# A decoder block on one core: first loads on two DMA queues, both layer norm borders in a written order, and the second norm turned as the first

## Chip, core and metric

The kernel runs on one core of a Trainium2 chip. TensorE (PE, with its weight loads as PEld), VectorE (DVE), ScalarE (ACT), GpSimd (POOL) and SyncE (SP) each run their own queue in order and meet through semaphores. The metric is the device time of one execution in microseconds (us), lower is better.

## What is computed

One layer of a decoder block on 256 tokens of width 2048, in float32:

```python
mix = token_mixers(x, w_in[i], ...)               # linear attention + softmax attention, two branches
x = layer_norm(ALPHA * x + mix, ln1_g[i], ln1_b[i])
ffn = conv_gated_mlp(x, w_gate[i], w_up[i], conv_w[i], conv_b[i], w_down[i])
x = layer_norm(ALPHA * x + ffn, ln2_g[i], ln2_b[i])
x = x + jax.nn.sigmoid(x @ w_ple_gate[i]) * (p[i] @ w_ple_proj[i])
```

`layer_norm` takes mean and variance over the 2048 columns of a token, scales by a gain `g` and adds a bias `b` per column.

## The kernel before

**Split products.** A float32 value is used as two parts of the PE's reduced format: ACT copies `raw` into `hi`, DVE subtracts to get `lo`, and a product is three matmuls (hi by hi, lo by hi, hi by lo). Weights come as units of 128 x 2048 in the order of use (`wu`): unit 120 to 135 are the output projection `wo`, 136 to 223 gate and up, 224 to 267 the down projection `dn`, 268 to 283 the last gate `pg`. `prep` (line 158) issues one unit's two loads on SP, one ACT copy (line 107, through `copy`) and one DVE subtraction (line 171) for each half. `unit` (line 179) hands out a unit and prepares two ahead.

**Order.** Only SP's order is that of the program (`tc.manual_schedule`, line 109). On the other engines a scheduler orders the instructions at build time by priority (`tc.high_priority`) and by its own costs; `tc.keep_in_program_order` pins single ones. On the chip each engine then runs its list in order. PE too is written by hand inside `end1`.

**Start.** SP loads the transposed input (`load_x`, line 192) and the first weights `fv` (`fv_prep`, line 393, with loads and splits on lines 401 to 403) in turn: k-tile 0 of the input (128 x 256), the first weight tile in three pieces (384, 384 and 280 columns), k-tile 1, the next weight tile in three pieces, and then whole tiles of 524 KB. For each, ACT makes `hi`, DVE makes `lo`. PE runs nine warm-up products (line 117) and then the `fv` products (line 426): 18 for each of 16 k-tiles.

**The norm borders.** `residual` (line 921) adds a projection's result to the residual `z`, in two halves of 1024 columns and two token tiles t of 128. The last two units of the second half are its tail. As each of the four tail banks (t, c) ends, DVE adds it to `z` (line 934 or 932) and takes statistics (line 935). After the two banks of a token tile come a few 1-column operations (on DVE, and one power on POOL), then, for each of four column groups g of 512:

- norm: scale by mean and deviation. On ACT one instruction; or on DVE;
- turn: four 128x128 transposes on PE into one of **two** PSUM banks (`pmx`, line 68), gain and bias, then `hi` by ACT and `lo` by DVE into `x1T[g]` or `x2T[g]`, which the next products read.

In the first border (`ln_steps`, line 870) groups 0 and 2 (`AFF_DVE`) get gain and bias before they are turned, by two DVE instructions over 512 columns with the gains laid out along columns (`lnb`, lines 889 and 891), so that the turned bank is split directly (ACT copy, DVE line 785). Groups 1 and 3 are turned plain: after the transposes four 128-column instructions take turns on ACT (line 911) and DVE (line 913), one bank, one after the other; then the ACT copy and the DVE difference (line 916). In the second border (`ln_out`, line 836) all four groups are turned plain (lines 862 and 864), one is normed on DVE (line 849), three on ACT (line 852).

To cover the borders PE has other work: the tail of the second token tile, a small product `pp` of the per-layer embedding (24 products of 512 columns: `proj` in `end1`, `ple_proj` in the second border), and the first products of the next stage by token halves (`phase0` needs token tile 0 alone, `phase1` token tile 1; in the second border the head units of `pg`, whose k-tiles 0 to 3 lie in `x2T[0]`). After the second border `affine` (line 966) adds gain and bias to `z2` on DVE for the final residual, two passes a group.

Of the kernel before, what the change touches and what calls it, by code (L numbers as in the profile page):

```python
# [19 lines left out]
P = 128  # L20
D = 2048
S = 256
# [14 lines left out]
ZN_DVE = (0,)  # L37
AFF_DVE = (0, 2)
LN_ORDER = (1, 0, 3, 2)
# [7 lines left out]
DNW = (DNP, DNP[:-1])  # L47
WH = 1152
# [7 lines left out]
def tile_block(ctx: ExitStack, tc: tile.TileContext, wu, wfv, wpp, xT_in, x_in, pT_in, wlr,  # L56
# [53 lines left out]
    nc.scalar.preload_act_table_set("natural_log_exp_and_others")  # L110
# [5 lines left out]
    for _ in range(9):  # L116
        nc.tensor.matmul(pw_, lhsT=warm[:, 0:P], rhs=warm, start=True, stop=True)
# [5 lines left out]
    sums, half = {}, {}  # L123
# [34 lines left out]
    def prep():  # L158
        u = n_prep[0]
        n_prep[0] += 1  # L160
        if u in sums:
            prep_seven(u)
            return
        his, los = [], []
        for h in range(2):
            raw = ring.tile([P, 1024], F32, tag="raw", bufs=4, name=f"raw{u}_{h}")
            nc.sync.dma_start(raw, wu[u, :, h * 1024:(h + 1) * 1024])
            hi = w_tile("hi", F32R, f"hi{u}_{h}", u)
            copy(hi, raw)
            lo = w_tile("lo", F32R, f"lo{u}_{h}", u)  # L170
            nc.vector.tensor_tensor(lo, raw, hi.bitcast(F32), ALU.subtract)  # L171
            his.append(hi)
            los.append(lo)
        ready[u] = (his, los)
# [4 lines left out]
    def unit():  # L179
        u = n_used[0]  # L180
        n_used[0] += 1
        while n_prep[0] < min(NU, u + 3):
# [9 lines left out]
    def load_x(g, k0, k1, step=2):  # L192
        for k in range(k0, k1, step):
            e = slice(k, k + step)
            raw = t2("xraw").rearrange("p (k t) -> p k t", t=S)[:, 0:step, :]
            nc.sync.dma_start(raw, xT_in[:, 4 * g + k:4 * g + k + step, :])
# [127 lines left out]
    def x_half(name, act, K, evac, pulls=0, head=0, tail=0, mid=None, done=None, end=None,  # L324
               fine=False, ws=(), joined=None):
# [15 lines left out]
        for t in range(2):  # L341
            for i, w in enumerate(us):
                mm(i, w, (t,))
# [49 lines left out]
    def fv_prep(u, hs=(0, 1), his=None, los=None):  # L393
        his, los = his or [], los or []
        for h in hs:
            raw = wide.tile([P, WH], F32, tag="hi", name=f"fvraw{u}_{h}")[:, 0:NS]
            hi = s8([P, NS], F32R, name=f"fvhi{u}_{h}")
            lo = s8([P, NS], F32R, name=f"fvlo{u}_{h}")
            for o, n in fch if u == 0 else ((0, NS),):
                e = slice(o, o + n)  # L400
                nc.sync.dma_start(raw[:, e], wfv[u, :, h, e])
                copy(hi[:, e], raw[:, e])
                nc.vector.tensor_tensor(lo[:, e], raw[:, e], hi[:, e].bitcast(F32), ALU.subtract)
# [432 lines left out]
    def ln_out(zs, stats, t, act_out, cg, cb, nm, prio):  # L836

        z = zs[t]
        mv = sm.tile([P, 8], F32, tag="mv", name="mv")
        with tc.high_priority(P_STAT):  # L840
            nc.vector.bn_aggr(mv[:, 0:2], stats[t])
            nc.vector.tensor_scalar(mv[:, 2:3], mv[:, 1:2], LN_EPS, None, ALU.add)
            nc.gpsimd.tensor_tensor(mv[:, 3:4], mv[:, 2:3], mhalf, ALU.pow)
            nc.vector.tensor_scalar(mv[:, 4:5], mv[:, 0:1], -1.0, mv[:, 3:4], ALU.mult, ALU.mult)
        with tc.high_priority(prio):
            for g in range(4):
                zc = z[:, g * 512:g * 512 + 512]
                if g in ZN_DVE:
                    nc.vector.tensor_scalar(zc, zc, mv[:, 0:1], mv[:, 3:4], ALU.subtract,
                                            ALU.mult)  # L850
                else:
                    nc.scalar.activation(zc, zc, AF.Identity, scale=mv[:, 3:4], bias=mv[:, 4:5])
                pt = mxtile(f"pt{nm}{t}{g}")
                for i in range(4):
                    nc.tensor.transpose(pt[:, i * P:i * P + P], zc[:, i * P:i * P + P], ident)
                y = t2("lny").rearrange("p (k t) -> p k t", t=P)
                for i in range(4):
                    kt = 4 * g + i
                    gc, bc = chn[:, cg + kt:cg + kt + 1], chn[:, cb + kt:cb + kt + 1]
                    src = pt[:, i * P:i * P + P]  # L860
                    if i % 2:
                        nc.scalar.activation(y[:, i, :], src, AF.Identity, scale=gc, bias=bc)
                    else:
                        nc.vector.tensor_scalar(y[:, i, :], src, gc, bc, ALU.mult, ALU.add)
                hi = act_out[g][:, :, t * P:t * P + P]
                copy(hi, y)
                nc.vector.tensor_tensor(act_out[g][:, :, 256 + t * P:256 + t * P + P], y,
                                        hi.bitcast(F32), ALU.subtract)

    def ln_steps(zs, stats, t, act_out, gb_, cg, cb, nm):  # L870
# [13 lines left out]
        def norm(g):  # L884
            e = slice(g * 512, g * 512 + 512)
            zc = z[:, e]
            with tc.high_priority(P_LN1[t]):
                if g in AFF_DVE:
                    nc.vector.scalar_tensor_tensor(zc, zc, mv[:, 0:1], gb_[0][:, e],
                                                   ALU.subtract, ALU.mult)  # L890
                    nc.vector.scalar_tensor_tensor(zc, zc, mv[:, 3:4], gb_[1][:, e],
                                                   ALU.mult, ALU.add)
                else:
                    nc.scalar.activation(zc, zc, AF.Identity, scale=mv[:, 3:4], bias=mv[:, 4:5])

        def turn(g):
            zc = z[:, g * 512:g * 512 + 512]
            with tc.high_priority(P_LN1[t]):
# [22 lines left out]
    def residual(name, act, K, zs, stats, mid, done=None, end=None, ws=((), ())):  # L921

        for nh in range(2):
# [4 lines left out]
            def ev(t, c, ps, nh=nh, zp=zp):  # L928
                zc = zp(t, c)
                with tc.high_priority(P_STAT):  # L930
                    if ws[nh]:
                        nc.vector.tensor_tensor(zc, zc, ps, ALU.add)
                    else:
                        nc.vector.scalar_tensor_tensor(zc, zc, ALPHA, ps, ALU.mult, ALU.add)
# [66 lines left out]
    def ple_proj(half, w, pTs):  # L1001
        banks = [[[mmtile(f"pp{half}{t}{c}")] for c in range(2)] for t in range(2)]
        for k in range(2):
            o = slice(k * 1024, k * 1024 + 1024)
            x_mm(banks, (w[0][:, o], w[1][:, o]), pTs[k], (0, 1), k == 0, k == 1)
        return banks

# [12 lines left out]
    def end1(tail_mm):  # L1020
# [3 lines left out]
        with tc.manual_schedule(engines={mybir.EngineType.PE}):  # L1024
# [8 lines left out]
            def put(t):  # L1033
                for c in range(2):
                    o = t2("ppo")
                    copy(o, pb[t][c][0])
# [4 lines left out]
            def phase0(i):  # L1041
                us.append(unit())
# [11 lines left out]
            stat0, norm0, turn0 = ln_steps(z1, st1, 0, x1T, gain[0], c_g1, c_b1, "l1")  # L1054
            stat1, norm1, turn1 = ln_steps(z1, st1, 1, x1T, gain[0], c_g1, c_b1, "l1")
# [19 lines left out]
            turn0(G[3])  # L1075
            proj(1, 1)
            put(1)
            for i in range(3):
                phase0(i)
                turn1(G[i])  # L1080
                if i == 0:
                    for g in G[2:]:
                        norm1(g)
            for j in range(4):
                phase1(j)
                if j == 0:
# [5 lines left out]
                         [g for g in range(4) if g not in AFF_DVE]))  # L1092
# [95 lines left out]
    residual("dn", hT, NF, z2, st2, ({14: lambda: mid2(0), 15: lambda: mid2(1)}, {8: mid2a, NF // 2 - 5: mid2b}), done2, ws=DNW)  # L1188
# [4 lines left out]
    mixers.append(affine(z2, gain[1], lambda t: None))  # L1193
# [7 lines left out]
    for nh in range(2):  # L1201
        def ev_o(t, c, ps, ab=(0, 512), nh=nh):
# [13 lines left out]
               fine=nh == 1)  # L1216
# [36 lines left out]
def _layout(i):  # L1253
# [16 lines left out]
    wfv = wfv.reshape(8, 2, P, NS).transpose(0, 2, 1, 3)  # L1270
# [17 lines left out]
    return dict(wu=wu, wfv=wfv, wpp=_xst(i["w_ple_proj"][0]), xT=x.T.reshape(16, P, S).transpose(1, 0, 2),  # L1288
# [23 lines left out]
```

## Time and profile before

| | us |
|---|---|
| median of 3 runs | 1663.86 (1661.83 to 1664.18) |
| the profiled execution's own time | 1663.05 |
| its span in the trace | 1661.3 |
| PE busy | 1650.9 |
| DVE busy | 1193.2 |
| ACT busy | 865.4 |
| read from and written to HBM | 332.33 MB, 9.97 MB |

A row of the timeline gives the start in us from the start of the span, the busy time, the engine, the source line, the operation, output and inputs, shapes, the count of merged instructions, and in brackets the idle time of the engine before it with what ended it. Matmuls are pipelined: a row of n products lasts n starts plus the time of the last to come out.

### The profile page before, as it was taken

What the parts mean: (1) busy time and instruction counts of PE and PEld (TensorE: products, weight loads), DVE (VectorE), ACT (ScalarE), POOL (GpSimd) and SP (SyncE); (2) the same over time, 40 slices, a digit from 0 to 9 for tenths busy, and PEclk for the clock granted to TensorE, in tenths of its full rate; (3) what the DMA queues carried; (4) which work ended last, traced back from release to release, by engine and by line L of the source; (5) the groups of instructions that cost most, each with busy time, mean ns of one, the idle gap of its engine ahead of it and who ended that gap; (6) DMA issues with size and microseconds to landing.
All of it is one profiled execution on the core that took longest, in us unless ns stands there. A gap on an engine that the chain in (4) does not pass through costs nothing.

```text
span 1661.3 us, 24083 instructions
## 1 busy us (share of the span) xinstructions
PE 1650.9 (99%) x8984; PEld 1432.3 (86%) x8984; DVE 1193.2 (72%) x1751; ACT 865.4 (52%) x1245; POOL 62.8 (4%) x175
## 2 busy tenths in 40 slices
PE   9999999999999999999999999999999999999998
PEld 8988888888888888888888888888888888888787
DVE  6666658768756657775677777777777788887874
ACT  6745445445555544544465555555555555454733
POOL 0000000000000000000010000000000011010000
PEclk9999999999999999999999999999999999999999
DMA  7665555555555555667746666666666667695554
GB/s 295 232 201 183 165 188 181 177 179 177 184 178 174 173 189 194 194 195 283 235 150 209 231 232 205 206 211 205 205 209 205 202 246 271 223 345 208 183 192 168
DMA packets 95588, 343.87 MB, mean 207 GB/s; under 512 B 11064, under 2 KB 12736, under 8 KB 94064
## 3 DMA queue, kind: packets, MB, share of 16 engines
q1 hardware_dynamic: 90528, 324.51, 58.3%
q0 software_dynamic: 4944, 17.84, 2.8%
q8 instruction: 70, 1.15, 0.3%
q14 instruction: 46, 0.38, 0.1%
HBM read 332.33 MB, written 9.97 MB: 206 GB/s over the span
## 4 chain that ended last, share of the span: by engine, by line
PE 94%; DVE 2%; DMA 2%; ACT 1%; issue 1%; SPq 0%; POOL 0%; DVEq 0%; ACTq 0%
PE psu L237 9%; PE psg L237 9%; PE psm L237 7%; PE dn L281 7%; PE gr L281 5%; PE gv L281 5%; PE wo L281 5%; PE psu L239 5%; PE psg L239 5%; PE pg L281 4%; PE psm L239 4%; PE psa L237 3%; PE fv L426 2%; PE psfq L237 2%; PE psfk L237 2%; PE psq L237 2%
## 5 line engine op out<-in xcount | busy, mean ns | idle before, releaser
L107 ACT ACTIVATE hi<-raw 128x1024 fp32r<-128x1024 f32 (+1 forms) x568 | 593.0, 1047 | 629.2 <-issue 217.0
L171 DVE TENSOR_TENSOR lo<-raw,hi 128x1024 fp32r<-128x1024 f32 x534 | 653.1, 1225 | 358.1 <-ACT hi L107 357.1
L237 PE MATMUL psu<-x1T,hi 128*128 128x512 f32 x688 | 236.0, 389 | 0.0
L237 PE MATMUL psg<-x1T,hi 128*128 128x512 f32 x672 | 230.5, 389 | 0.0
L239 PE MATMUL psu<-x1T,lo 128*128 128x256 f32 x688 | 190.0, 276 | 0.0
L239 PE MATMUL psg<-x1T,lo 128*128 128x256 f32 x672 | 185.5, 276 | 0.0
L237 PE MATMUL psm<-xT,hi 128*128 128x512 f32 x512 | 175.8, 391 | 0.0
L237 PEld LDWEIGHTS psu<-x1T,hi 128*128 128x128 f32 x688 | 129.2, 188 | 26.7
L237 PEld LDWEIGHTS psg<-x1T,hi 128*128 128x128 f32 x672 | 126.2, 188 | 26.1
L239 PE MATMUL psm<-xT,lo 128*128 128x256 f32 x512 | 141.5, 276 | 0.0
L239 PEld LDWEIGHTS psu<-x1T,lo 128*128 128x128 f32 x688 | 129.1, 188 | 0.0
L239 PEld LDWEIGHTS psg<-x1T,lo 128*128 128x128 f32 x672 | 126.2, 188 | 0.0
L281 PE MATMUL dn<-hi,hT 128*128 128x512 f32 x432 | 121.4, 389 | 0.0
L237 PEld LDWEIGHTS psm<-xT,hi 128*128 128x128 f32 x512 | 96.2, 188 | 19.8
L239 PEld LDWEIGHTS psm<-xT,lo 128*128 128x128 f32 x512 | 96.2, 188 | 0.1
L281 PEld LDWEIGHTS dn<-hi,hT 128*128 128x128 f32 x432 | 81.0, 188 | 16.8 <-ACT hi L107 0.2
L237 PE MATMUL psa<-oT,hi 128*128 128x512 f32 x256 | 87.8, 389 | 0.0
L281 PE MATMUL gv<-hi,xT 128*128 128x512 f32 x256 | 72.3, 394 | 0.0
L281 PE MATMUL gr<-hi,xT 128*128 128x512 f32 x256 | 72.2, 394 | 0.0
L239 PE MATMUL psa<-oT,lo 128*128 128x256 f32 x256 | 70.7, 276 | 0.0
L281 PE MATMUL wo<-hi,mT 128*128 128x512 f32 x256 | 70.2, 390 | 0.0
L281 PE MATMUL dn<-lo,hT 128*128 128x512 f32 x216 | 68.9, 391 | 0.6 <-DVE lo L171 0.5
(300 smaller groups left out, 2806.2 us busy)
## 6 DMA issues: line engine op xcount, KB each, us to landing
raw<-in_wu_dram SPq DMA_DIRECT2D x568, 512.0 KB, 4.7
fvraw<-in_wfv_dram SPq DMA_DIRECT2D x14, 524.0 KB, 7.9
hi<-hsd POOLq DMA_DIRECT2D x17, 256.0 KB, 5.1
lo<-hsd POOLq DMA_DIRECT2D x17, 256.0 KB, 5.3
lnb<-in_lng_dram SPq DMA_DIRECT2D x4, 1024.0 KB, 9.0
hsd<-hsh POOLq DMA_DIRECT2D x9, 256.0 KB, 5.7
hsd<-hsl POOLq DMA_DIRECT2D x9, 256.0 KB, 5.5
z<-in_x_dram SPq DMA_DIRECT2D x2, 1024.0 KB, 8.5
```

The source lines that it names most:

```text
L107: nc.scalar.activation(o, i, AF.Copy, bias=0.0, scale=scale)
L171: nc.vector.tensor_tensor(lo, raw, hi.bitcast(F32), ALU.subtract)
L237: nc.tensor.matmul(ps, lhsT=hi[i // 8 if hoff == 0 else 0][:, w0 % 1024:w0 % 1024 + P], rhs=a[:, kt % 4, :], start=first and i == 0, stop= ...
L239: nc.tensor.matmul(ps[:, 256:512], lhsT=lo[i // 8 if hoff == 0 else 0][:, w0 % 1024:w0 % 1024 + P], rhs=a[:, kt % 4, 0:256], start=False, ...
L281: nc.tensor.matmul(bs[j][:, 0:m], lhsT=x, rhs=v[:, o:o + m], start=first and i == 0, stop=last and i == 2)
L426: nc.tensor.matmul(fbk[t][c][:, 0:n], lhsT=x, rhs=w[:, o:o + n], start=kt == 0 and i == 0, stop=kt == 15 and i == 2)
```

## The change

**Start.** The first weight tile now comes as its first 384 columns (`w0`), issued by ACT ahead of everything else there, while SP issues k-tile 0 (`x0`) and then one load of 920 columns (`w1`: k-tile 1 and the other 664 weight columns). The second weight tile is one load. The host lays these out in one array (`xw`), and lays `wfv` and `xT` out so that each load is one contiguous piece. Eight warm-up products stand in place of nine.

**First border.** The four tail banks run through without transposes between them, token tile 1's norms are pinned behind token tile 0's turns, the `lo` parts of units 137 and 138 are moved to written places, units 139 and 140 are prepared after the border, and the last turn stands one step later.

**Second border.** `ln_out` goes; `ln_steps` serves both. So groups 0 and 2 are scaled once by DVE before they are turned, groups 1 and 3 on ACT and turned plain. PE's order is written by hand there too: tail, then a quarter of `pp` and a turn of token tile 0, four times, then a head product of `pg` and a turn of token tile 1, four times. The norms of token tile 1 and the preparation of units 270 and 271 are pinned. `affine` for `z2` keeps to groups 1 and 3.

```diff
-ZN_DVE = (0,)
 AFF_DVE = (0, 2)
+PLAIN = (1, 3)
+LATE_LO = (137, 138)
+PIN = (270, 271)
+PIN_LO = (270, 271)
...
+    w0 = wide.tile([P, 1024], F32, tag="lo", name="w0")[:, 0:384]
+    nc.scalar.dma_start(w0, xw[256 * P:640 * P].rearrange("(p n) -> p n", n=384))
...
-    for _ in range(9):
+    for _ in range(8):
...
-    load_x(0, 0, 1, 1)
-    f0 = fv_prep(0, (0,))
-    load_x(0, 1, 2, 1)
-    fvu = [fv_prep(0, (1,), *f0)]
+    x0 = t2("xraw")[:, 0:256]
+    nc.sync.dma_start(x0, xw[0:256 * P].rearrange("(p n) -> p n", n=256))
+    w1 = wide.tile([P, 1024], F32, tag="lo", name="w1")[:, 0:920]
+    nc.sync.dma_start(w1, xw[640 * P:].rearrange("(p n) -> p n", n=920))
...
+    x_split(0, x0)
+    fv_split(*f0, w0, slice(0, 384))
+    fv_split(*f0, w1[:, 256:920], slice(384, NS))
+    x_split(1, w1[:, 0:256])
+    f1 = fv_prep(0, (1,))
...
-            for i in range(2):
-                tail_mm(1, 0, i)
-            tail_mm(1, 1, 0)
+            for c in range(2):
+                for i in range(2):
+                    tail_mm(1, c, i)
             turn0(G[0])
-            tail_mm(1, 1, 1)
+            proj(0, 0)
             turn0(G[1])
             stat1()
             for g in G[2:]:
                 norm0(g)
-            proj(0, 0)
+            proj(1, 0)
             turn0(G[2])
-            proj(1, 0)
-            put(0)
-            for g in G[:2]:
-                norm1(g)
             proj(0, 1)
             turn0(G[3])
+            norm1(G[0], keep)
+            norm1(G[1], keep)
+            put(0)
+            low(u1, 0)
+            norm1(G[2], keep)
             proj(1, 1)
             put(1)
...
-    def done2(t):
-        if t == 1:
-            pb.extend(ple_proj(1, *pq[0]))
-        ln_out(z2, st2, t, x2T, c_g2, c_b2, "l2", P_LN2[t])
+    def end2(tail_mm):
...
+        for g in range(2, 4):
+            norm0(g)
+        stat1()
...
+        for g, (k, t) in enumerate(((0, 0), (0, 1), (1, 0), (1, 1))):
+            proj(k, t)
+            turn0(g)
+        for g in range(4):
+            norm1(g, tc.keep_in_program_order)
+
+    def begin3(mm):
+        turn1, = late_turns
+        for g, (i, t) in enumerate(((0, 0), (1, 0), (0, 1), (1, 1))):
+            mm(i, t)
+            turn1(g)
+        border.close()
```

How the built programs order this, at three places. First the DVE queue in the first border, from token tile 1's last statistics on; `z_7195` (before) and `z_7184` (after) are token tile 1, `x1T_7196` to `x1T_7199` and `x1T_7185` to `x1T_7188` column groups 0 to 3. Before:

```order
L878 BN_AGGR mv<-st_85 128x2
L916 TENSOR_TENSOR x1T_7197<-lny,x1T_7197 128x4x128
L879 TENSOR_SCALAR mv<-mv 128x1
L785 TENSOR_TENSOR x1T_7196<-ptl_7850,x1T_7196 128x4x128
L881 TENSOR_SCALAR mv<-mv 128x1
L913 TENSOR_SCALAR lny<-ptl_7870,chn 128x128
L889 SCALAR_TENSOR_TENSOR z_7195<-z_7195,mv,lnb_7422 128x512 x2
L913 TENSOR_SCALAR lny<-ptl_7870,chn 128x128
L891 SCALAR_TENSOR_TENSOR z_7195<-z_7195,mv,lnb_7423 128x512 x2
L916 TENSOR_TENSOR x1T_7199<-lny,x1T_7199 128x4x128
L785 TENSOR_TENSOR x1T_7198<-ptl_7903,x1T_7198 128x4x128
```

After:

```order
L921 TENSOR_TENSOR x1T_7186<-lny,x1T_7186 128x4x128
L823 TENSOR_TENSOR x1T_7185<-ptl_7843,x1T_7185 128x4x128
L918 TENSOR_SCALAR lny<-ptl_7863,chn 128x128 x2
L921 TENSOR_TENSOR x1T_7188<-lny,x1T_7188 128x4x128
L823 TENSOR_TENSOR x1T_7187<-ptl_7881,x1T_7187 128x4x128
L893 SCALAR_TENSOR_TENSOR z_7184<-z_7184,mv,lnb_7411 128x512
L895 SCALAR_TENSOR_TENSOR z_7184<-z_7184,mv,lnb_7412 128x512
```

The four norm instructions of token tile 1 (line 889 and 891) stood between the third group's turned pieces and the last two differences of token tile 0; now all of token tile 0 stands ahead of the first pair, and the second pair follows later.

Second, the DVE queue in the second border after the change, from token tile 1's aggregate on; `z_12836` is token tile 1, `x2T_12838` to `x2T_12841` groups 0 to 3, `ptl_14709` the bank of token tile 0's fourth turn, `ptl_14773` that of token tile 1's first:

```order
L882 BN_AGGR mv<-st_12837 128x2
L823 TENSOR_TENSOR x2T_12838<-ptl_14665,x2T_12838 128x4x128
L883 TENSOR_SCALAR mv<-mv 128x1
L918 TENSOR_SCALAR lny<-ptl_14678,chn 128x128
L885 TENSOR_SCALAR mv<-mv 128x1
L180 TENSOR_TENSOR lo_1_14579<-raw_1_14575,hi_1_14577 128x1024
L918 TENSOR_SCALAR lny<-ptl_14678,chn 128x128
L921 TENSOR_TENSOR x2T_12839<-lny,x2T_12839 128x4x128
L823 TENSOR_TENSOR x2T_12840<-ptl_14696,x2T_12840 128x4x128
L918 TENSOR_SCALAR lny<-ptl_14709,chn 128x128 x2
L921 TENSOR_TENSOR x2T_12841<-lny,x2T_12841 128x4x128
L893 SCALAR_TENSOR_TENSOR z_12836<-z_12836,mv,lnb_14103 128x512
```

And before, from a little behind the same point; `z_12847` is token tile 1, `x2T_12849` to `x2T_12852` groups 0 to 3:

```order
L864 TENSOR_SCALAR lny<-ptl_14652,chn 128x128
L844 TENSOR_SCALAR mv<-mv 128x1
L867 TENSOR_TENSOR x2T_12849<-lny,x2T_12849 128x4x128
L864 TENSOR_SCALAR lny<-ptl_14652,chn 128x128
L864 TENSOR_SCALAR lny<-ptl_14665,chn 128x128
L867 TENSOR_TENSOR x2T_12850<-lny,x2T_12850 128x4x128
L849 TENSOR_SCALAR z_12847<-z_12847,mv 128x512
```

Token tile 1's norm of group 0 on DVE (one instruction, line 849) stood ahead of the last differences of token tile 0; now it is two (lines 893 and 895) and stands behind token tile 0's very last one.

Third, SP's first rows, before:

```order
L196 DMA xraw<-in_xT_dram 128x256
L401 DMA fvraw_0_128<-in_wfv_dram 128x384 x2
L401 DMA fvraw_0_128<-in_wfv_dram 128x280
L196 DMA xraw<-in_xT_dram 128x256
L401 DMA fvraw_1_144<-in_wfv_dram 128x384 x2
L401 DMA fvraw_1_144<-in_wfv_dram 128x280
L196 DMA xraw<-in_xT_dram 128x512
L401 DMA fvraw_0_160<-in_wfv_dram 128x1048
```

After, where ACT's first row is a load as well (`w_90`, 384 columns):

```order
L434 DMA xraw<-in_xw_dram 128x256
L436 DMA w_129<-in_xw_dram 128x920
L426 DMA fvraw_1_139<-in_wfv_dram 128x1048
L214 DMA xraw<-in_xT_dram 128x512
L426 DMA fvraw_0_149<-in_wfv_dram 128x1048
```

Ahead of the third weight tile (`fvraw_0_160`, now `fvraw_0_149`) SP issued nine loads, and now four.

More of the change, by code (lines that the diff above doesn't have):

```diff
@@ L121, in tile_block @@
     ready = {}
-    sums, half = {}, {}
+    sums, half, later = {}, {}, {}
     def prep_seven(u):
@@ L177, in tile_block, with unit @@
     NU = wu.shape[0]
-    def unit():
+    def unit(ahead=3):
         u = n_used[0]
         n_used[0] += 1
-        while n_prep[0] < min(NU, u + 3):
+        while n_prep[0] < min(NU, u + ahead):
             prep()
@@ L340, in x_half @@
         us = [unit() for _ in range(head)]
-        for t in range(2):
-            for i, w in enumerate(us):
-                mm(i, w, (t,))
+        if begin is not None:
+            begin(lambda i, t: mm(i, us[i], (t,)))
+        else:
+            for t in range(2):
+                for i, w in enumerate(us):
+                    mm(i, w, (t,))
         for i in range(head, n - tail):
@@ L834, in tile_block, with ln_steps @@
     ppd = dr.tile([2, P, 1024], F32, name="ppd")
[L836 to L870, printed above, removed]
+    def ln_steps(zs, stats, t, act_out, gb_, cg, cb, nm, prio):
         z = zs[t]
```

151 lines of the change are left out of this document (101 added, 50 removed).

## The prediction, made blind

> **What bounds the kernel now.** I read the shares of the span on the profile's first page, then what PE waited for by line, then the timeline at the three places that the change touches.
>
> ```profile
> span 1661.3 us, 24083 instructions
> PE 1650.9 (99%) x8984; PEld 1432.3 (86%) x8984; DVE 1193.2 (72%) x1751; ACT 865.4 (52%) x1245; POOL 62.8 (4%) x175
> ...
> PE fv L426 <- ACT fvhi L107: 1.7, 1, 1.7
> ...
> PE psg L250 <- DVE x1T L916: 1.1, 1, 1.1
> PE ptl L855 <- DVE z L849: 0.9, 1, 0.9
> PE dn L281 <- DVE lo L171: 0.5, 1, 0.5
> ```
>
> PE is busy 99% of the span and the change leaves its products as they are (one warm-up product less). So only PE's waits can move the time, and the list has them all in a few rows: one at the start, one in the first border, two in the second. What is to be won is about 5 us of 1663, and what can be lost is whatever new wait the written order makes.
>
> The prices of a product come from two rows of the chain of work (start, length, count): `fv` products have 384, 384 or 280 columns, those of `pg` 512.
>
> ```profile
> 13.62 39.12 PE fv L426 x246
> ...
> 1572.26 38.12 PE pg L281 x168
> ```
>
> A mean `fv` product costs 39.12/246 = 0.159, a 512-column product 38.12/168 = 0.227, and one of 256 columns half of that, 0.113.
>
> **A, the start.**
>
> ```profile
> 1.19 3.57 PE L117 MATMUL warm_ps<-warm 128*128 128x512 bf16 x9 [1.19 <-DVE warm L114]
> 2.92 0.42 ACT L107 ACTIVATE xT<-xraw 128x256 fp32r<-128x256 f32 x1 [0.58 <-DMA xraw<-in_xT_dram]
> 3.65 0.52 ACT L107 ACTIVATE fvhi<-fvraw 128x384 fp32r<-128x384 f32 x1 [0.32 <-DMA fvraw<-in_wfv_dram]
> 4.41 0.53 PE L426 MATMUL fv<-fvhi,xT 128*128 128x384 f32 x1
> ...
> 10.38 0.29 PE L426 MATMUL fv<-fvhi,xT 128*128 128x280 f32 x1
> 11.21 1.08 ACT L107 ACTIVATE fvhi<-fvraw 128x1048 fp32r<-128x1048 f32 x1 [1.17 <-DMA fvraw<-in_wfv_dram]
> 12.33 1.22 PE L426 MATMUL fv<-fvhi,xT 128*128 128x384 f32 x6 [1.66 <-ACT fvhi L107]
> 2.00:4.00 2.00, 2.00 (x6) 0.76 (x5) 0.43 (x1) 1.09 (x4) 0.00 (x0) 1.00 0.90 283
> 4.00:6.00 2.00, 2.00 (x11) 1.48 (x10) 1.12 (x2) 1.04 (x3) 0.00 (x0) 1.00 0.87 256
> 6.00:8.00 2.00, 2.00 (x15) 1.99 (x14) 1.70 (x4) 1.47 (x4) 0.00 (x0) 1.00 0.98 245
> 12.00:14.00 2.00, 1.60 (x8) 1.33 (x9) 1.63 (x2) 1.78 (x3) 0.00 (x0) 1.00 1.05 424
> ```
>
> (The last four rows are stretches of 2 us; their last column is what the DMA engines moved, in GB/s.) PE had done the 36 products of the first two k-tiles and stood still until the third weight tile had landed at 11.21 and been copied. From 13.62 on, 246 of the 288 products run without a gap. The six ahead of them, without a gap too, would start at 13.62 - 6 x 0.159 = 12.67: that is the effective start of k-tile 2 before.
>
> After, the first product comes at about 4.35: `x0` and `w0` are issued side by side and land at 3.3 to 3.7, near where ACT's copies found them before, and with eight warm-up products PE is free then. The 36 products take 36 x 0.159 = 5.72, and I add 0.5 for the wait on `w1`, now one load of 471 KB in place of three small ones. So k-tile 2 may begin at 10.6. Does its weight tile land in time? Up to its end 2,134 KB have to come. While the rows were of 1,024 to 1,536 bytes the engines moved 245 to 283 GB/s at a busy share of 0.87 to 0.98, and 424 at the same share when the rows were 4,192 bytes. After the change nearly all rows are 3,680 or 4,192 bytes: 566 KB in 2 to 4 us at the first stretch's 283, the other 1,568 KB at 424 in 3.7, thus landed near 8, copied by 9.2, no wait. A = 10.6 - 12.67 = **-2.0** (rounded up a little). Bounds: if no wait is left among the 36 products and the first comes at 4.1, -2.8; if the rate stays near 250, the tile lands at 2.0 + 2,134/250 = 10.5 instead of 11.21, -0.6.
>
> The Trainium skill's page "DMA: Bandwidth & Descriptors", section "Issuing engines are not separate DMA queues", speaks against the first half of this edit: transfers started by ScalarE, SyncE or GpSimd run on the same 16 engines and interleave, and starting them on several engines saves only the issue time, which it calls usually small. The rows above, with engines busy 0.87 and more from 2 us on, agree with it. By that rule the second queue alone is worth one issue on SP, and the rest of A must come from the larger rows.
>
> **B, the first border.**
>
> ```profile
> 836.95 0.42 PEld L901 LDWEIGHTS ptl<-ident,z 128*128 128x128 f32 x4 [0.50 <-ACT z L894]
> 840.69 0.42 PEld L901 LDWEIGHTS ptl<-ident,z 128*128 128x128 f32 x4 [0.30 <-DVE lny L913]
> 844.25 1.41 DVE L889 SCALAR_TENSOR_TENSOR z<-z,mv,lnb 128x512 f32<-128x512 f32 x2
> 845.89 1.41 DVE L891 SCALAR_TENSOR_TENSOR z<-z,mv,lnb 128x512 f32<-128x512 f32 x2
> 847.21 0.69 DVE L916 TENSOR_TENSOR x1T<-lny,x1T 128x512 fp32r<-128x512 f32 x1
> 847.96 1.35 PE L250 MATMUL psg<-x1T,hi 128*128 128x256 f32 x8 [1.13 <-DVE x1T L916]
> 849.50 2.13 PE L250 MATMUL psu<-x1T,hi 128*128 128x256 f32 x16
> ```
>
> Three waits: 0.50 before the first transposes, 0.30 for a PSUM bank, and 1.13 for `x1T` of the fourth group, which stood on DVE behind the four norm instructions of token tile 1 (1.41 + 1.41). Together 1.93. After, all of token tile 0 stands ahead of those four, and 24 products of 512 columns lie between the turns, so the 1.13 goes; the 0.50 goes as the whole tail of token tile 1 now stands before the first turn (6 x 0.227 = 1.36 more cover). The norms of token tile 1 come late instead: its first turn has `phase0`'s 48 products of 256 columns ahead of it, 48 x 0.113 = 5.4, against two instructions of 0.74, and its last one stands a `phase1` step later, which hides the late pair too. At the turns a bank wait stays: two banks for four turns, and ACT still has weight copies of 1.04 in its queue between the 128-column pieces. I take 0.6 for that, twice the 0.30 seen. B = 0.6 - 1.93 = **-1.3**, bounds -1.9 (nothing waits) and 0 (the bank waits take all back).
>
> **C, the second border.**
>
> ```profile
> 1556.06 1.06 ACT L107 ACTIVATE hi<-raw 128x1024 fp32r<-128x1024 f32 x1 [2.78 <-PE dn L281]
> 1558.48 1.09 PE L855 MATMUL ptl<-ident,z 128*128 128x128 f32 x8 [0.87 <-DVE z L849]
> 1559.47 0.72 DVE L864 TENSOR_SCALAR lny<-ptl,chn 128x128 f32<-128x128 f32 x2
> 1559.92 0.81 ACT L862 ACTIVATE lny<-ptl,chn 128x128 f32<-128x128 f32 x2 [0.28 <-DVE lny L864]
> ...
> L171 DVE TENSOR_TENSOR lo<-raw,hi 128x1024 fp32r<-128x1024 f32 x6 | 7.2, 1224 | 3.0 <-ACT hi L107 3.0
> ...
> L913 DVE TENSOR_SCALAR lny<-ptl,chn 128x128 f32<-128x128 f32 x8 | 3.3, 412 | 1.5 <-ACT lny L911 1.4
> ...
> L889 DVE SCALAR_TENSOR_TENSOR z<-z,mv,lnb 128x512 f32<-128x512 f32 x4 | 2.9, 746 | 0.0
> L891 DVE SCALAR_TENSOR_TENSOR z<-z,mv,lnb 128x512 f32<-128x512 f32 x4 | 2.9, 746 | 0.0
> ...
> L916 DVE TENSOR_TENSOR x1T<-lny,x1T 128x512 fp32r<-128x512 f32 x4 | 2.7, 674 | 0.7 <-ACT x1T L107 0.7
> L107 ACT ACTIVATE x1T<-lny 128x512 fp32r<-128x512 f32 x4 | 2.5, 630 | 0.5 <-DVE lny L913 0.5
> ...
> L862 ACT ACTIVATE lny<-ptl,chn 128x128 f32<-128x128 f32 x16 | 6.8, 468 | 0.3 <-DVE lny L864 0.3
> ```
>
> Before, PE loses the 0.87 of the `ptl` row here (the 0.5 at `dn` comes from a late weight load and stays). After, the whole tail of token tile 1 covers the first norm, so that 0.87 goes. But token tile 1's first norm, the DVE pair of lines 893 and 895, now stands behind the fourth turn's difference on DVE. The chain from the fourth turn's transposes: ACT piece 0.468, DVE piece 0.412, again 0.468 and 0.412, ACT copy 0.63, DVE difference 0.674, norm 0.746 and 0.746: 4.56, with eight hand-overs of about 0.04 (ACT's copy at 11.21 ended at 12.29 and PE began at 12.33) some 4.85. PE meanwhile has one head product, 12 matmuls of 512 columns, 12 x 0.227 = 2.72, and then needs that `z`: it stands 2.1, up to 2.6 if ACT first copies the third bank; I take 2.5. Behind PE at that point stand all head products of `pg`, so nothing else fills the hole. At the fourth turn's bank I expect 0.6 more: the second turn's pieces have a `lo` of 1.22 between them on DVE, about 3.8 in all, while two quarters of `pp` and one turn cover 2 x 6 x 0.227 + 0.42 = 3.14. C = 2.5 + 0.6 - 0.87 = **+2.2**. Bounds: all of it hidden -0.9; two late banks and 3.3 at the first turn +3.3.
>
> **The rest, at 0.** Eight passes fewer in `affine`, the moved `lo` parts and later units are on DVE, ACT and SP, behind which PE has two units in hand (two times 24 x 0.227); if that cover were gone, a `lo` would cost its 1.2. The tail of the program is as before. Sum: -2.0 - 1.3 + 2.2 = -1.1. The profiled execution took 1663.05 (its span 1661.3 and 1.75 around it), so 1661.95 for it; the median of the runs was 0.81 above it, so **1662.7**.
>
> **Rivals.**
>
> R1, the pieces do not alternate. In the rows at 1559.47 and 1559.92 DVE and ACT each run two pieces back to back, 0.72 and 0.81, in part side by side. If that holds for the fourth turn, the four pieces take about 0.85 instead of 1.9, the stall is 1.1, the bank wait goes, C = 1.1 - 0.87 = +0.2: 1663.86 - 3.1 = 1660.8; with nothing left, 1659.7. Against it, the first border:
>
> ```profile
> 849.78 0.46 ACT L911 ACTIVATE lny<-ptl,chn 128x128 f32<-128x128 f32 x1 [1.65 <-PE ptl L901]
> ...
> 851.13 0.46 ACT L911 ACTIVATE lny<-ptl,chn 128x128 f32<-128x128 f32 x1 [0.90 <-DVE lny L913]
> ```
>
> There ACT's second piece of one bank waited 0.90 for DVE's piece.
>
> R2, **slower than before**: in ACT's queue the copy of unit 269's second half stands ahead of every piece of the turns, and it waits for its load.
>
> ```profile
> 1550.63 1.06 ACT L107 ACTIVATE hi<-raw 128x1024 fp32r<-128x1024 f32 x1 [2.55 <-DMA raw<-in_wu_dram]
> ```
>
> A copy waited 2.55 for its load only 8 us ahead of the turns. If that copy is late, all turns are late by as much, with no other cover than the `pp` quarters; from 1.1 of lateness on the sum is positive, and at 2.55 it is +1.5: 1665.3. Against it: the copy at 1556.06 waited for PE, not for its load.
>
> R3, the start does not do what it says: the rate stays as it was, A = -0.6, sum +0.3: 1664.2. For it: the engines were already busy at 0.90 in the row of 2 to 4 us. Against it: 424 GB/s with long rows. The Trainium skill's section named above speaks for it too.
>
> **How the numbers follow.** The forecast, 1662.7, gets 0.60 (its own range 1660.8 to 1664.6), R1 0.21, R2 0.09, R3 0.10. The range reaches from R1's lower end, 1659.7, to a little above R2, 1665.6. A difference under 0.2%, 3.3 us, is about what a measurement of this kernel cannot tell from no change; so faster means under 1660.5 (nearly half of R1 and the forecast's good ends, A at -2.8 with B at -1.9: 0.22), slower above 1667.2 (R2 with bad ends: 0.05), and 0.73 is left for no change.
>
> **What would show it.** A: no gap of PE between 10 and 13 us, and `fv`'s chain ends at 50.7 instead of 13.62 + 39.12 = 52.74. B: the wait of `psg` for `x1T` is gone from the list. C: a wait of `ptl` for DVE's `z` of 2 to 3 us behind the first head product of `pg`. If that row is short, R1 holds; if a turn's pieces begin behind a copy that waits for a load, R2 does; if ACT waits for the third weight tile as late as 10 us, R3. Wrong altogether it would be if a wait stood anywhere between the borders.

## The result, and the profile after

The changed kernel takes **1665.99 us** (median of 20 runs, 1664.33 to 1668.72), the kernel before 1663.11 in the same runs (1661.83 to 1664.18): ratio **1.0019**, 95% interval 1.0012 to 1.0026. It is slower by 2.9 us. The forecast was 1662.7, 1.1 under the median then shown (1663.86, of three runs; the median of twenty is 0.75 lower); the time lies 0.4 over the range's upper end. The profiled execution after took 1665.31, 2.26 more than that of before.

The page's head and PE's waits by line, after:

```profile
span 1663.5 us, 24041 instructions
PE 1652.4 (99%) x8983; PEld 1433.0 (86%) x8983; DVE 1189.9 (72%) x1738; ACT 861.4 (52%) x1232; POOL 63.7 (4%) x175
...
PE ptl L906 <- issue: 2.7, 1, 2.7
PE dn L299 <- DVE lo L180: 1.0, 2, 0.7
PE ptl L906 <- DVE mv L883: 0.9, 1, 0.9
PE ptl L906 <- DVE lny L918: 0.3, 1, 0.3
PE dn1m L320 <- DVE ts L159: 0.2, 1, 0.2
PE ptl L906 <- DVE x1T L823: 0.2, 1, 0.2
```

The waits of before at `fv` and at `psg` are gone, and three of the transposes (`ptl`) have come, all in the second border. "issue" means that the profile found no releaser.

**Start.** The timeline of PE, ACT and DVE after:

```profile
4.28 0.82 PE L464 MATMUL fv<-fvhi,xT 128*128 128x384 f32 x1
5.36 0.84 PE L464 MATMUL fv<-fvhi,xT 128*128 128x384 f32 x2
7.05 1.08 ACT L110 ACTIVATE fvhi<-fvraw 128x1048 fp32r<-128x1048 f32 x1 [0.73 <-DMA fvraw<-in_wfv_dram]
8.16 1.25 DVE L416 TENSOR_TENSOR fvlo<-fvraw,fvhi 128x1048 fp32r<-128x1048 f32 x1 [0.93 <-ACT fvhi L110]
8.28 1.24 PE L464 MATMUL fv<-fvhi,xT 128*128 128x280 f32 x7
9.47 0.19 PEld L464 LDWEIGHTS fv<-fvlo,xT 128*128 128x128 f32 x1 [0.17 <-DVE fvlo L416]
```

The chain of work has all of `fv` in one row (start, length, count):

```profile
4.78 47.10 PE fv L464 x288
```

And two stretches by windows, with GB/s last:

```profile
4.00:6.00 2.00, 2.00 (x7) 1.42 (x5) 0.82 (x2) 0.97 (x3) 0.00 (x0) 1.00 0.94 344
6.00:8.00 2.00, 2.00 (x12) 2.00 (x12) 1.19 (x2) 1.27 (x3) 0.00 (x0) 1.00 1.03 400
```

The loads did get faster, 344 and 400 GB/s against 256 and 245 in the same stretches. But `fv` is done at 4.78 + 47.10 = 51.88 instead of 52.74: 0.86 earlier, not 2.0. The limit is now the *second* weight tile: it lands at 7.05, whole, is copied until 8.13 and subtracted until 9.41. PE's products of k-tile 1 begin at 8.41, right behind k-tile 0 (the last six of the row at 8.28; the first of it closes k-tile 0). These six need only the copy. The next one needs the difference and starts at 9.47, and the rest of `fv` follows it without another wait.

**First border.** One wait is left there, and it is the bank wait that was expected:

```profile
843.09 0.66 PE L906 MATMUL ptl<-ident,z 128*128 128x128 f32 x4 [0.18 <-DVE x1T L823]
...
869.90 0.39 PE L255 MATMUL psg<-x1T,hi 128*128 128x512 f32 x1
```

The second row is the 109th product of `psg`, a mark behind the border. Before, the same product started here:

```profile
872.04 0.39 PE L237 MATMUL psg<-x1T,hi 128*128 128x512 f32 x1
```

It comes 2.14 earlier; less the 0.86 of the start, the border gives 1.28.

**Second border.** PE, DVE and ACT, after:

```profile
1562.94 0.66 PE L906 MATMUL ptl<-ident,z 128*128 128x128 f32 x4 [0.89 <-DVE mv L883]
1565.33 0.66 PE L906 MATMUL ptl<-ident,z 128*128 128x128 f32 x4 [0.34 <-DVE lny L918]
1571.46 0.63 PE L906 MATMUL ptl<-ident,z 128*128 128x128 f32 x4 [2.70 <-issue]
1560.96 1.21 DVE L180 TENSOR_TENSOR lo<-raw,hi 128x1024 fp32r<-128x1024 f32 x1
1562.26 0.63 DVE L823 TENSOR_TENSOR x2T<-ptl,x2T 128x512 fp32r<-128x512 f32 x1
1563.74 1.21 DVE L180 TENSOR_TENSOR lo<-raw,hi 128x1024 fp32r<-128x1024 f32 x1
1569.22 0.69 DVE L921 TENSOR_TENSOR x2T<-lny,x2T 128x512 fp32r<-128x512 f32 x1 [0.69 <-ACT x2T L110]
1569.83 0.75 DVE L893 SCALAR_TENSOR_TENSOR z<-z,mv,lnb 128x512 f32<-128x512 f32 x1
1570.61 0.75 DVE L895 SCALAR_TENSOR_TENSOR z<-z,mv,lnb 128x512 f32<-128x512 f32 x1
1560.70 0.46 ACT L916 ACTIVATE lny<-ptl,chn 128x128 f32<-128x128 f32 x1 [1.05 <-PE ptl L906]
1563.30 0.46 ACT L916 ACTIVATE lny<-ptl,chn 128x128 f32<-128x128 f32 x1 [2.14 <-DVE lny L918]
1567.62 0.46 ACT L916 ACTIVATE lny<-ptl,chn 128x128 f32<-128x128 f32 x1 [0.84 <-DVE lny L918]
```

At 1571.46 PE waits 2.70 for token tile 1's first norm; the DVE pair at 1569.83 and 1570.61 ends at 1571.36, and it stands where the order had it, behind the fourth turn's difference at 1569.22. At 1562.94 the third turn waits 0.89 for its bank: the difference that empties it (1562.26) stands on DVE behind a `lo` of 1.21. (The row names line 883, a 1-column operation that DVE ran right behind that difference.) At 1565.33 the fourth waits 0.34 for the second turn's pieces, of which DVE's last stands behind the second `lo`. ACT's two pieces at 1560.70 and 1563.30 belong to one bank, and the piece at 1567.62 is the second of the fourth turn: the pieces do alternate.

The last `pg` product, started at 1655.32 before, starts at 1657.38. So 2.06 = -0.86 (start) - 1.28 (first border) + **4.20** (all behind it). Of the 4.20 the three waits are 3.93 less the 0.87 of before. Each wait also costs about 0.16 more than its idle time (from product start to product start the three are late by 1.06, 0.51 and 2.86), and there are two more of them than before; and the waits of `dn` for `lo` grew from 0.5 to 1.0. That makes about 3.9; the rest of the 4.20 is not accounted for.

### The profile page after: what moved, and what is told of

Read it like the earlier page. It is cut to its first block, busy times and chain, and to the rows that moved or that the text cites. A ratio compares the mean times of both kernels' runs of the same rounds, so it can differ in the third digit from the quotient of the medians.

```text
span 1663.5 us, 24041 instructions
## 1 busy us (share of the span) xinstructions
PE 1652.4 (99%) x8983; PEld 1433.0 (86%) x8983; DVE 1189.9 (72%) x1738; ACT 861.4 (52%) x1232; POOL 63.7 (4%) x175
## 4 chain that ended last, share of the span: by engine, by line
PE 94%; DVE 2%; DMA 1%; issue 1%; ACT 1%; POOL 0%; POOLq 0%; SPq 0%; DVEq 0%; ACTq 0%
PE psu L255 9%; PE psg L255 9%; PE psm L255 7%; PE dn L299 6%; PE gr L299 5%; PE gv L299 5%; PE wo L299 5%; PE pg L299 5%; PE psu L257 5%; PE psg L257 5%; PE psm L257 4%; PE psa L255 3%; PE fv L464 3%; PE psfq L255 2%; PE psfk L255 2%; PE psq L255 2%
## 5 line engine op out<-in xcount | busy, mean ns | idle before, releaser
L174 ACT ACTIVATE hi<-raw 128x1024 fp32r<-128x1024 f32 x534 | 564.7, 1060 | 598.2 <-issue 215.6
```

The source lines that it names most:

```text
L174: c = nc.scalar.activation(hi, raw, AF.Copy, bias=0.0, scale=1.0)
```

## Experiments

All times below are against the kernel before, run on the same chip; an interval is 95%. One 0.001 of ratio is 1.66 us. The changed kernel itself has 1.0019; where a run is set beside it, two such ratios are compared.

### Parts undone

**a1: the second border of before**, the other two parts changed. Edit (and what belongs to it: `ple_proj`, `affine` over all groups, no pins):

```diff
-    def end2(tail_mm):
...
-    def begin3(mm):
...
+    def done2(t):
+        if t == 1:
+            pb.extend(ple_proj(1, *pq[0]))
+        ln_out(z2, st2, t, x2T, c_g2, c_b2, "l2", P_LN2[t])
```

> The changed kernel with the second border of the kernel before (start and first border stay changed). Theory (the loss is all in the second border, the other two parts gain what the two traces show, 0.86 at the start and 1.16 at the first border): 2.0 us under before, ratio 0.9988, and PE's waits between 1530 and 1585 back at about 2.5 us in all. Rival (the parts disturb each other, or the gains of the profiled execution are chance): within 0.7 us of before.

Ratio 0.9997 (0.9988 to 1.0006). Its profiled span is 1660.0, and the waits in its second border are those of `ln_out`:

```profile
PE ptl L894 <- DVE z L888: 1.9, 2, 1.6
```

The loss against before is gone, so it was in the second border. The gain of 2.0 is not shown: it is the far end of the interval, and the medians differ by 0.14 alone, as the rival has it. Part of the reason stands in the row: its second border waits 1.9 for the norm, in two waits, where the kernel before waits 0.87, and 1.20 in its second profile (b0).

**b0: the kernel before, again.**

> The kernel before once more, for a second profile of its start. If the start of the one profile is typical, PE's third weight tile is waited for by 1.6 to 1.9 us again and the last fv product starts near 52.4; if executions differ there by more than 0.5 us, the 0.86 between the two first profiles is no measure of the change.

1663.94. Its chain of work has the row

```profile
13.75 39.12 PE fv L426 x246
```

`fv` done at 52.87, beside 52.74 (the wait for the third tile was only 0.8 this time, as PE came to it later). In eight profiles with the changed start and the whole second tile on two queues (the changed kernel twice, a1 to a4, b1, c5) it is done at 51.88, 52.56, 52.41, 52.21, 52.44, 52.76, 53.12 and 52.63: 52.5 in the mean. The second tile landed at 7.05 in the first of them and between 7.54 and 8.29 in the others. So the start gains about **0.3**, and the 0.86 of the first profile was a good draw. The gain of the first border, by contrast, is between 1.2 and 1.3 in every profile.

### The start

**a2: nine warm-up products.** Edit: `range(8)` to `range(9)`.

> The changed kernel with nine warm-up products, as before, in place of eight. In the trace after, the first fv products run 0.32 us apart for 384 columns until 6.5 us, in the trace before 0.17 to 0.18 from 5.1 us on. Theory W (the pause of PE between the eighth warm-up and the first product keeps PE slow): full speed from about 5 us, 1 us under the changed kernel, about 1.9 over before. Rival (the moment of full speed is a matter of chance or of when products pause later on): products slow until past 6 us again in the profile, time as the changed kernel, 2.9 over before.

Ratio 1.0011 (1.0002 to 1.002); the products were slow until 6.6 again. Over all profiles the slow first products come and go with eight warm-ups (slow in the changed kernel's first profile, a1 and a4, not in a3, b1 or c1) and with nine (slow in a2 and b0, not in the first profile of before). They do not set the end: a1 has them and is done at 52.41, a3 has not and is done at 52.44, as PE then only waits longer for k-tile 1. Theory W falls.

**b3: the second weight tile split in pieces.** One load still:

```diff
-            fv_split(hi, lo, raw, slice(0, NS))
+            for o, n in fch if (u, h) == (0, 1) else ((0, NS),):
+                fv_split(hi, lo, raw[:, o:o + n], slice(o, o + n))
```

> The changed kernel, but the second weight tile, still one load, is copied and subtracted in three pieces of 384, 384 and 280 columns, as before. Theory (the start lost its gain because k-tile 1's products wait for a copy of 1.08 and a subtraction of 1.25 of a whole tile that lands at 7.0 to 7.6): k-tile 1's first product at 7.6 to 8.1 in place of 8.4 to 9.1, fv done 0.4 to 0.8 earlier. Rival (PE's slow first products or the landing itself set the start): first product of k-tile 1 and end of fv as in the changed kernel, 51.6 to 52.4.

ACT in the timeline of this kernel (the three pieces as one row):

```profile
7.59 1.26 ACT L110 ACTIVATE fvhi<-fvraw 128x384 fp32r<-128x384 f32 x3 [1.64 <-DMA fvraw<-in_wfv_dram]
```

Its chain of work:

```profile
8.76 43.18 PE fv L465 x269
```

K-tile 1 starts at 8.16 and `fv` is done at 51.94, although the tile landed only at 7.59. The two other kernels with the pieces (c1, c2) are done at 51.61 and 51.60. Their mean is 51.7, 0.8 earlier than with the whole tile. Not all of this is the pieces: in c1 and c2 the tile also landed earlier than in most of the eight, at 7.23 and 6.70. With the same landing (7.60 in a3, 7.59 here) the end is 52.44 whole and 51.94 in pieces. So the theory holds, and the pieces are worth about 0.5; why the landing differs from execution to execution, no run shows. The time, 1.0012 (1.0003 to 1.0021), lies under the changed kernel's 1.0019, but the intervals overlap.

**b4: one queue.** `w0` is issued by SP behind `x0`:

```diff
-    nc.scalar.dma_start(w0, xw[256 * P:640 * P].rearrange("(p n) -> p n", n=384))
...
+    nc.sync.dma_start(w0, xw[256 * P:640 * P].rearrange("(p n) -> p n", n=384))
     w1 = wide.tile([P, 1024], F32, tag="lo", name="w1")[:, 0:920]
```

> The changed kernel, but w0 is issued by SP behind x0, so that one queue makes all first loads. Theory (the second queue saves one issue of about 0.4, and that is hidden behind the wait for the second weight tile): first fv product up to 0.4 later, k-tile 1's first product and the end of fv as in the changed kernel, time the same. Rival (two queues make the loads themselves faster): landings of w1 and of the second weight tile later by more than 0.5, fv done more than 0.5 later.

PE's first product in the timeline, and `fv` in the chain of work:

```profile
4.22 0.67 PE L464 MATMUL fv<-fvhi,xT 128*128 128x384 f32 x1
```

```profile
10.36 42.42 PE fv L464 x264
```

The first product is not later (4.22; 4.28 to 4.45 with eight warm-ups and two queues), `fv` is done at 52.78, within what two queues gave. Ratio 1.0016 (1.0007 to 1.0025), as the changed kernel. No use of the second queue can be seen. This agrees with the Trainium skill ("DMA: Bandwidth & Descriptors", section "Issuing engines are not separate DMA queues"), by which a second issuing engine saves only the time of issuing.

### The second border

**a3: the norm earlier.**

```diff
             proj(k, t)
+            if g == 3:
+                norm1(0, tc.keep_in_program_order)
             turn0(g)
-        for g in range(4):
+        for g in range(1, 4):
             norm1(g, tc.keep_in_program_order)
```

> The changed kernel, but token tile 1's first norm (two DVE instructions) is pinned ahead of the fourth turn's pieces instead of behind its difference. Theory (the stall of 2.7 us before token tile 1's first turn is that place in DVE's queue): the stall falls to 0.3 to 1.0, 2 us under the changed kernel, about 0.9 over before. Rival (DVE has no room in this border whatever the order): what is taken from that wait comes back at the next turns or at the fourth turn's bank, within 0.7 of the changed kernel.

Ratio 0.9994 (0.9985 to 1.0003). PE and DVE:

```profile
1569.55 0.63 PE L906 MATMUL ptl<-ident,z 128*128 128x128 f32 x4 [0.61 <-issue]
1567.72 0.74 DVE L893 SCALAR_TENSOR_TENSOR z<-z,mv,lnb 128x512 f32<-128x512 f32 x1
1568.70 0.74 DVE L895 SCALAR_TENSOR_TENSOR z<-z,mv,lnb 128x512 f32<-128x512 f32 x1
```

The pair now runs between the fourth turn's pieces and ahead of its difference. The wait falls from 2.70 to 0.61, with the same two waits at the third and fourth turn (0.90 and 0.34). One place in DVE's queue was worth 2.1 us of the trace. The time came down to that of before, where 0.9 over it was expected; c4 has a part of the reason.

**a4: unit 269's `lo` later**, behind token tile 1's first norms (through the kernel's own list `LATE_LO`).

```diff
-LATE_LO = (137, 138)
+LATE_LO = (137, 138, 269)
...
             norm1(g, tc.keep_in_program_order)
+            if g == 1:
+                for rest in later[269]:
+                    with tc.high_priority(P_LN2[1]):
+                        tc.keep_in_program_order(rest())
```

> The changed kernel, but both lo parts of unit 269 stand on DVE behind token tile 1's first norm, not between token tile 0's turns. Theory (the 0.9 to 1.06 at the third turn and the 0.3 to 0.5 at the fourth are banks held because of these two subtractions of 1.2): both waits go, the stall before token tile 1's first turn stays near 2.7, and up to 0.5 comes at the second head product's lo; 1 to 1.5 us under the changed kernel. Rival (the banks wait for ACT's pieces or token tile 1's statistics): both waits stay above 0.7 in sum, within 0.5 of the changed kernel or slower, as lo is then late.

Ratio 1.001 (1.0001 to 1.0019).

```profile
1563.74 0.66 PE L906 MATMUL ptl<-ident,z 128*128 128x128 f32 x4 [0.47 <-DVE lny L918]
...
1569.87 0.84 PE L906 MATMUL ptl<-ident,z 128*128 128x128 f32 x4 [2.72 <-issue]
```

The third turn's wait is gone, the fourth's is 0.47, in sum 0.47 for 1.23; the stall stays at 2.72. The `lo` parts did hold the banks. By ratio the gain over the changed kernel is 1.5 us, as expected, but the intervals overlap; the profiled execution lost some of it behind the stall, see c4.

**b1: both, with one `lo` ahead of the norm.**

```diff
+            if g == 3:
+                low(0)
+                norm1(0, tc.keep_in_program_order)
             turn0(g)
+        low(1)
```

> The changed kernel with token tile 1's first norm ahead of the fourth turn's pieces, and unit 269's lo parts moved: the first ahead of that norm, the second behind the fourth turn's difference. Theory (DVE's work in this border is near what PE's cover leaves, so that moving lo only moves the wait): the waits at the third and fourth turn fall from 1.6 to 0.6, that before token tile 1's first turn rises from 0.7 to about 1.2; the border within 0.5 us of the kernel with the early norm alone. Rival (the two remedies add): another 1.0 to 1.5 us less than with the early norm alone, then under before.

Ratio 0.9994 (0.9985 to 1.0003), as a3.

```profile
1569.70 0.63 PE L906 MATMUL ptl<-ident,z 128*128 128x128 f32 x4 [1.72 <-issue]
```

The two bank waits together are 0.1, for 1.24 in a3, and the stall has grown from 0.61 to 1.72: what was taken there came back here. The border of the changed kernel as one stretch by windows (busy times of PE, PEld, DVE, ACT, POOL):

```profile
1557.00:1571.40 14.40, 10.53 (x53) 7.85 (x51) 12.11 (x23) 8.33 (x15) 0.55 (x1) 1.00 0.26 83
```

DVE is busy 12.1 of 14.4 us, PE 10.5 (the other 3.9 are its three waits): here DVE's queue, not PE's, is the longer one.

**c2: more cover on PE.** With b1's early norm and b3's pieces (the second `lo` now ahead of the fourth turn's difference), both head products of token tile 0 stand ahead of the first two turns of token tile 1:

```diff
-        for g, (i, t) in enumerate(((0, 0), (1, 0), (0, 1), (1, 1))):
-            mm(i, t)
-            turn1(g)
+        mm(0, 0)
+        mm(1, 0)
+        turn1(0)
+        turn1(1)
+        mm(0, 1)
+        turn1(2)
+        mm(1, 1)
+        turn1(3)
```

> The changed kernel with the pieces at the start, the early norm, unit 269's lo parts on both sides of that norm, and PE's order in the second border changed: both first-half head products ahead of token tile 1's first two turns, so that 24 instead of 12 matmuls cover its norm. Theory (the loss is cover against DVE's chain): the stall before token tile 1's first turn falls to 0.5 or less, a new wait of 0.3 to 1.0 for its split comes before the next head product, the second border as before within 0.7; 1 to 2 us under before. Rival (DVE's queue is late by itself): the stall stays over 1.5.

Ratio **0.999** (0.9982 to 0.9999).

```profile
1569.43 0.74 PE L299 MATMUL pg<-lo,x2T 128*128 128x512 f32 x2 [1.00 <-DVE lo L180]
...
1571.76 0.73 PE L299 MATMUL pg<-hi,x2T 128*128 128x512 f32 x2 [0.25 <-ACT x2T L110]
```

No turn waits for the norm any more, and the split costs 0.25 (the fourth turn still waits 0.46 for its bank). The 1.00 in its place is DVE again: PE has reached the second head unit's `lo` before DVE has. The three waits sum to 1.71, as much as b1's 1.72 and more than the 0.87 and 1.20 of before. From the 109th `psg` product to the last of `pg` this kernel takes 785.64, and the kernel before 783.28 and 784.02 in its two profiles. So the stall went as forecast, but the stretch did not come back to that of before: the wait moved on to `lo`, and the gain in time is that of the start and the first border. (Three things differ from b1 here, so the cover alone is not measured.)

**c5: a longer queue.** Both `lo` parts pinned between the fourth difference and the norm:

```diff
+        for rest in later[269]:
+            with tc.high_priority(P_LN2[1]):
+                tc.keep_in_program_order(rest())
         for g in range(4):
             norm1(g, tc.keep_in_program_order)
```

> The changed kernel with both lo parts of unit 269 pinned ahead of token tile 1's first norm, behind the fourth turn's difference: it lengthens the stall by two subtractions of 1.2. Theory (the stall is the length of DVE's queue between the fourth turn and the norm): stall 2.9 + 2.4 = 5.3, the waits at the third and fourth turn down to 0.6 as when lo stood elsewhere, so 1 to 2 us over the changed kernel; and if a longer idle time always slows PE, seven or more head products 0.427 apart behind it, another 1.4 to 3. Rival (the stall is not that queue): stall near 2.9.

Ratio 1.0029 (1.0018 to 1.0041).

```profile
1572.51 1.09 PE L906 MATMUL ptl<-ident,z 128*128 128x128 f32 x4 [5.02 <-issue]
```

5.02 for 2.70: 2.3 more, which is two subtractions of 1.2. The stall follows the length of that queue.

**c4: the changed kernel, again.**

> The changed kernel once more, for a second profile. In its first profile the head products behind the stall of 2.9 run 0.227 us apart; with the stall as long, two other kernels had eight of them 0.427 apart. If that is chance in each execution, this profile shows the one or the other with the same waits ahead of it; the time is 2 to 4.5 us over before.

1666.92. PE behind the same stall, in the timeline:

```profile
1571.68 0.63 PE L906 MATMUL ptl<-ident,z 128*128 128x128 f32 x4 [2.74 <-issue]
1572.06 1.08 PE L299 MATMUL pg<-hi,x2T 128*128 128x512 f32 x2
1572.94 1.05 PE L299 MATMUL pg<-lo,x2T 128*128 128x512 f32 x2
1573.79 1.91 PE L299 MATMUL pg<-hi,x2T 128*128 128x512 f32 x4
```

The stretch by windows (the granted clock stands third from the end):

```profile
1572.00:1575.00 3.00, 3.00 (x10) 2.40 (x9) 2.22 (x4) 2.92 (x5) 0.00 (x0) 0.53 0.00 0
```

The granted clock is 0.53 and eight products start 0.427 apart instead of 0.227: 8 x 0.2 = 1.6 us on top of the stall. With stalls of 2.70 to 2.74, three profiles have this (c4, a4, b3) and three do not (the first of the changed kernel, a2, b4). The 20 runs of the changed kernel point the same way: the 5 with a mean granted clock of 1.000 took 1665.3 in the mean, the 15 with 0.999 or 0.998 took 1666.6. That is why the median after, 2.9 over before, can lie above the first profile's 2.3. The profiles of a3, b1 and c2, without such a stall, show no such products.

**c1: the parts that gained.** a1 and b3 together.

> The two parts that gained, without the one that lost: changed start with the second weight tile split in three pieces, changed first border, second border as before. By the traces so far: fv done 0.3 to 0.9 earlier, first border 1.25 less, second border 0: 1.6 to 2.1 us under before, ratio 0.9988 to 0.9990. Rival: executions differ more than that and the ratio is 1.000 within its interval.

Ratio **0.999** (0.9982 to 0.9999). Its second border waits 1.85 once:

```profile
1556.50 1.09 PE L895 MATMUL ptl<-ident,z 128*128 128x128 f32 x8 [1.85 <-DVE z L889]
```

That is 1.0 more than in the first profile of before at the same place and 0.65 more than in its second, which takes back part of what the start and the first border give; why it is longer, no run shows. c1 and c2 are both under both kernels, by 1.3 to 1.7 us against before (medians 1662.56 and 1662.45 for 1663.89, ratio 0.999); their intervals end just under 1.

## Why the prediction was wrong

- **A, the start: wrong in size, and for a reason it did not weigh.** Forecast -2.0, bounds -2.8 to -0.6; the mean of eight profiles is about -0.3. The step that failed is "I add 0.5 for the wait on `w1`": it made no term for the second weight tile, which had come in three pieces and now comes, and is split, whole. With the sum's own prices the 25th product, the first that as a rule needs this tile's difference, would start at 4.35 + 0.5 + 24 x 0.159 = 8.7; behind the landing, a copy of 1.08 and a subtraction of 1.25 it started at 9.5 to 10.7 in those profiles. The third tile, on which the sum looked, was copied in time, and the rate rose much as forecast (longer rows, contiguous pieces and fewer loads came together, and no run separates them). R3 had nearly the right number (-0.6) by luck: its mechanism, a rate that stays, did not occur.
- **B, the first border: right.** Forecast -1.3, measured -1.28 in the first profile, and -1.2 to -1.3 in every one. The size is partly luck. Two of its terms were each 0.4 too large and cancelled: the 0.50 and 0.30 of before were idle times of the weight loads, behind which PE's own products were late by 0.24 and less than 0.14, and the bank wait of after is 0.18 for the 0.6 taken.
- **C, the second border: right in mechanism and place, too small.** Forecast +2.2 with an upper bound of +3.3, measured +4.2 in the first profile. The stall itself was 2.70 for the 2.5 taken, and a3 and c5 show its cause. What failed is the step "at the fourth turn's bank I expect 0.6 more", as the only other wait: the wait of 0.89 at the **third** turn was missing, where the difference that empties the bank stands behind a `lo` (a4 takes it away; the upper bound allowed two late banks, the sum one, and the fourth turn took 0.34 for its 0.6). Also put at nothing were about 0.5 at `dn` and, in three of six profiles, 1.6 of half speed behind the stall.
- **The rest at 0** held: fewer passes of `affine` show in no wait.
- **R1 fell**: ACT's second piece of the second turn waited 2.14 for DVE's, that of the fourth 0.84. **R2 fell**: ACT's copy of unit 269's second half ran without a wait for its load.
- The sum was -2.0 - 1.3 + 2.2. From two profiles of each kernel, the stretch from that `psg` product to the last of `pg` is 783.28 and 784.02 before, 787.48 and 788.28 (with the half speed) after: +4.2 in the mean. So -0.3 - 1.3 + 4.2 = +2.6, beside +2.9 in the median. Two errors of the same sign, 1.7 and 2.0, carried it over the upper end of the range. What stays open is the waits of `dn` for `lo` parts of late loads, from none (a1) to 1.1 and different in each profile; no run took them apart.

## What to carry to other kernels

Where PE is full and an order is written by hand, add up the queue of the *other* engine between two points that PE must pass: the border turned on DVE having 12.1 us of work in 14.4. Moving the norm ahead took 2.1 of the stall away, but after that moving a `lo` only moved the wait with it (b1), and so did more cover on PE (c2). When several small loads are joined into one, price every tile that is joined, down to its copy and subtraction, not the last of them alone. And one profile of each side is a single draw: a place that varies by 0.5 us between executions needs several.

## What the runs showed of the hardware

- A PE idle for 2.72 to 2.74 us ran at half speed for some 3 us afterwards in three of six executions (the three others, idle for 2.70 to 2.74, did not), in the one with 5.02 too, and in none of the profiles whose longest stall there was 1.85 or less; the granted clock showed it (0.53 in c4). The Trainium skill, "TensorE: Matmul & The Clock Gate", section "What's actually happening", states half clock after an idle window of about 3.4 us that runs freely, which fits the chance, but not the length: 2.7 was enough here.
- At the kernel's start a speed nearly as low came and went between executions: in five of fourteen profiles products of 384 columns started 0.32 apart until 6.6 to 7.0 us, in the others 0.17 to 0.18 apart from 5.0 to 5.7 on. The profile's windows showed a granted clock of 1.00 in one of the slow ones too (the changed kernel's first, 4.2 to 6.4 us): there the distance of the products tells it, not that column.
